# One pair of key tiles for both layers and two more SBUF pieces, with the order of all engines redone

## The chip, the cores and the metric

The kernel runs on one core of one Trainium2 chip. The time is the device time of one execution in microseconds. The core has a matmul engine (TensorE, PE in the profile), three engines for everything else (VectorE or DVE, ScalarE or ACT, GpSimd or POOL) and a queue, SyncE or SP, that issues all the DMAs here. The matmuls' sums lie in PSUM, eight banks of 128 x 512 floats; all other tiles lie in SBUF, 128 partitions wide.

## The reference

One inference step of two layers, for a prompt of 512 tokens and for 8 sequences of one new token each with 512 tokens in caches. 520 tokens go through each layer together. The reference, cut to its frame:

```python
for l in range(DEPTH):                       # 2 layers; prompt and samples alike
    h = rmsnorm(x, w_norm[l])
    a_val, a_gate, z_a, b_in, z_b, q, kv, gate, z_c = split(h @ w_in[l])
    q = rope(rmsnorm(q, g_q));  k = rope(rmsnorm(k, g_k))          # 8 query, 2 key heads, 3 branches
    y_a = conv_mixer(a_val * sigmoid(a_gate))                      # depthwise width 31, layer norm, 256 x 256
    y_b = pool_mixer(b_in)                                         # trailing means over 2, 4, 8, 16
    o_c = attention over blocks compressed by a small MLP (32 rows, stride 16)
    o_s = attention over the 8 best blocks of 64 rows
    o_w = attention over a window of 256 rows
    o = gate0 * o_c + gate1 * o_s + gate2 * o_w
    x = x + concat(y_a * silu(z_a), y_b * silu(z_b), o * silu(z_c)) @ w_out[l]
```

For the prompt there are at most 8 blocks of 64 rows, so the selection takes all of them. For the samples the window, the compressed rows and the selected rows come from caches: `cache_win_kv`, and `cache_cmp_kv` and `cache_slc_kv` through a page table (4 pages of 128 rows for each sequence).

## The kernel before, in words

All values are kept with channels on the partitions and the 520 tokens along the row. A float32 product is made exact enough with two rounded halves: `split` (L727) writes the value rounded to float32r, the high half, and the rest, the low half; `product` (L747) then makes three matmuls of 128 x 128 weights by 260 tokens for each of two halves of the tokens, so a group of six for each of 8 input chunks, and 48 for one product of 128 output channels. Each product fills two PSUM banks. 24 such products for each layer are the input projection (`proj`, from `w_in`) and 8 the output (`out`, L1375, from `w_out`). The projections are made on x without its norm; `evac` (L761) multiplies their sums with the norm of each token when it takes them out of PSUM. That norm comes from `norm` (L780) and `spread` (L698): sums of squares on PE, a reciprocal root in ten small DVE operations, a store of the 520 values to DRAM (a tile called `rs`), and a read back to all partitions.

The steps of a layer (L1412) are: the norm; keys and values of three branches (`key`, `value`); the compression of cached pages (`cmp_pages` loads 16 pages for each of two halves of the sequences, `compress` is matmuls of 160 or fewer columns); queries; attention for four blocks of 128 prompt queries (`attend`, L1180); convolution and its layer norm (`conv_norm`, L1073); pooling; the decode for two times four sequences (`decode`, L1270); and the output products.

In `decode` four window tiles' loads (`in_win`) feed the scores `s2`, and 16 page loads (`in_slc`) the scores `s1`. DVE and ACT make the softmax of both; PE transposes the result (seven transposes, in two sets), copies of these out of PSUM are the weights of 28 products, and one last transpose gives the four sequences' rows.

`attend` reads the keys of the selected and of the window branch as one row of 1088 columns: 512 keys of a branch and 32 compressed ones, two times. `key` and `cmp` write them, as a high and a low half. Before, each layer has two such tiles of its own (L589, L797).

**What sets the order.** The program is first recorded, step by step, as 3,330 numbered units (`Plan.add`), each one instruction or a burst of matmuls. The table `"order"` (L395) is a permutation of those numbers, and every engine and the SP queue get their instructions in that order (`emit`, L326); each engine runs its own list strictly in order. A second table, `"engines"` (L386), has a letter for each of 776 operations that more than one engine can do (copies out of PSUM, roundings, subtractions, scalings): v for DVE, s for ACT, g for POOL (`Choice.put`, L168). `place` (L286) walks through the order and gives each tile a piece of a region of SBUF, or a PSUM bank, that is free at that point, the one that has been free longest. So the order also decides which earlier tile an operation waits for. The regions stand at L383, as width in columns and number of pieces: region b, of 1040 columns, holds the attention rows of `attend` (`pr`), the cache loads of `decode` (`kvt`), a tile of compressed values (`vcd`) and the compression weights (`w1`).

Of the kernel before, what the change touches and what calls it, by code (L numbers as in the profile page):

```python
# [9 lines left out]
F32R = mybir.dt.float32r  # L10
# [179 lines left out]
class Plan:  # L190
# [135 lines left out]
    def emit(self, tc, ctx):  # L326
# [27 lines left out]
L = 2  # L354
# [32 lines left out]
        "vsssvvssgsssgssssvsgsgvvsgvgsvsssvgvvsgvvgggssvvvssvgvsvvvvvsvvvvvsvvvvvgvvsvvvvvssgggsvvvvgsggvsvssgvvsvsgsgssg"  # L387
        "vvsgggsvssvvvsggsvsvvgsvsvsvggsgssvggvvvggsssgsvvsvsvggvgggsvsvvvvgsvsvsgvgsvggsvvgggssssssvsvvggsggvsgggggvsgsg"
        "gvssvgvgvgsvsgvsvsvvssssssssgvgsvsvgvgvvvvvgvvvvgvssggggsgsvsgsvgvsssvssvsssssssssgsggvvvgvvvggvvvssvvsvvvgsssss"
        "vsvsvsvsgsgggsvgvgvvgvsgsvsvvvvvsgsvvgvvsvvgvvsvvvvvsssvvgvvsvgsvvsvsgvgsgvvsggvvgssvsvvvggsvvggsssvvvggggsgvvvv"  # L390
        "svvvsvsvvsvsgvvgvvgvvssvvvvssgvvvgvvsgvvvgvsggvsvsvvvvsggvsvssvvvsvvgvgggvsvsvsgsgggvsssvgsvssvvgvvvvvsssvvvgsgg"
        "gsvggggvgsggvvssgvvsgsvgsvvsvsssvsvggsvvgvsggvvgvgsggsvssgssgsggssssvvssssvssvvvgggsvgvggggvgsvvvsggvgggssssvgsv"
        "svggsvvvvsssvvsvssvvssvvvgvggvvgvggvggssvssvsgsvssvssvvsggvvgvvsvgvvvvvgsgsvsgsvsvsvgvsgggsvvgsggvgvsgsg"
    ),
    "order": (  # L395
# [147 lines left out]
def step_kernel(ctx: ExitStack, tc: tile.TileContext, i, o, tune=None):  # L543
# [176 lines left out]
    def layer(l):  # L720
# [63 lines left out]
        def rotate(src, dst):  # L784
# [7 lines left out]
            else:  # L792
                ch("vg").tensor_tensor(dst[0], t[:, :S], sh[:, :S], OP.add)
                ve.tensor_tensor(dst[1], t[:, S:T], sh[:, S:T], op=OP.add)

        z_.vs = {}
        kh, kl = keys[l]  # L797

        def kv_tiles():
            z_.knew, z_.vnew = new("knew", [128, 2, NB]), new("vnew", [NB, 2, 128])  # L800
# [756 lines left out]
```

## Time and profile before

| | before |
|---|---|
| median of 3 runs | 615.49 us (615.11 to 616.38) |
| the profiled execution | 617.24 us |
| its span in the trace | 615.5 us |
| PE busy | 601.9 us, 98% |
| DVE, ACT, POOL busy | 451.9, 259.6, 205.8 us |
| DMA | 90.99 MB, mean 148 GB/s |
| TensorE's granted clock | full in all of 40 slices |

The span goes from the first to the last instruction of the trace; the rest of the execution lies around it. PE's matmuls overlap each other, so its busy time is the time in which at least one is under way. Where a row ends in brackets, they hold the time the engine stood still before it, and what ended that.

### The profile page before, as it was taken

The page shows a single profiled execution, that of the slowest core. Times are in us where ns is not written, and L with a number is a line of the kernel's source. Part 1 is how long each engine was busy: PE and PEld are TensorE (multiplying, and loading weights), DVE is VectorE, ACT ScalarE, POOL GpSimd, SP SyncE. Part 2 cuts the span into 40 slices and gives each one's busy share as a digit, 9 for nine tenths or more (in the row PEclk, how much of TensorE's full clock was granted, in tenths as well). Part 3 has the DMA queues.
Part 4 walks back from the last instruction along what each step waited for, and adds up shares of the span by engine and source line. Part 5 has one row for each costly group of instructions (what it writes and reads, how often), then busy time and mean ns, then how long its engine had stood idle before and what let it go on. Part 6 is the DMA issues. An engine that isn't in the chain of part 4 may idle for free.

```text
span 615.5 us, 15050 instructions
## 1 busy us (share of the span) xinstructions
PE 601.9 (98%) x5542; PEld 538.0 (87%) x5542; DVE 451.9 (73%) x1264; ACT 259.6 (42%) x736; POOL 205.8 (33%) x224
## 2 busy tenths in 40 slices
PE   9989999999999999999999999999999999998997
PEld 8988999998788797679999999999986969677997
DVE  5465899988768887874573698898987598798411
ACT  5001135586664965520110220327846878424100
POOL 2211325633452354040502023443441444523330
PEclk9999999999999999999999999999999999999999
DMA  8574554214742456774854632532245315878951
GB/s 283 165 227 134 179 162 151 87 60 109 175 96 79 122 165 210 229 233 145 160 186 151 190 105 85 161 104 72 67 115 124 87 49 147 210 242 256 184 138 69
DMA packets 89131, 90.99 MB, mean 148 GB/s; under 512 B 25858, under 2 KB 59746, under 8 KB 88930
## 3 DMA queue, kind: packets, MB, share of 16 engines
q1 hardware_dynamic: 89058, 90.04, 50.8%
q8 instruction: 43, 0.70, 0.5%
q14 instruction: 30, 0.25, 0.1%
HBM read 75.32 MB, written 14.67 MB: 146 GB/s over the span
## 4 chain that ended last, share of the span: by engine, by line
PE 49%; DVE 2%; DMA 2%; SPq 1%; ACT 1%; issue 1%; POOL 0%; DVEq 0%; POOLq 0%
PE banks L352 49%; DVE t L352 1%; DMA t<-in_win 1%; SPq L352 1%; ACT t L352 1%; DMA t<-in_w_out 1%; DVE small L352 1%; POOL t L352 0%; ACT small L352 0%; DVEq L352 0%; POOLq L352 0%
## 5 line engine op out<-in xcount | busy, mean ns | idle before, releaser
L352 PE MATMUL banks<-t,t 128*128 128x260 f32 (+5 forms) x3976 | 483.5, 300 | 2.8 <-DVE t L352 1.8
L352 PEld LDWEIGHTS banks<-t,t 128*128 128x128 f32 (+3 forms) x3976 | 435.3, 177 | 35.1 <-issue 24.7
L352 POOL TENSOR_TENSOR t<-t,t 128x512 fp32r<-128x512 f32 (+4 forms) x78 | 102.2, 1315 | 161.1 <-PE banks L352 67.8
L352 ACT ACTIVATE t<-t 128x512 fp32r<-128x512 f32 (+4 forms) x125 | 75.2, 616 | 157.7 <-DVE t L352 68.6
L352 ACT ACTIVATE t<-t,small 128x384 f32<-128x384 f32 (+4 forms) x188 | 100.2, 549 | 12.5 <-DVE small L352 11.4
L352 DVE TENSOR_TENSOR t<-t,t 128x512 fp32r<-128x512 f32 (+4 forms) x108 | 75.3, 708 | 19.3 <-POOL t L352 8.7
L352 PE MATMUL banks<-keep,t 128*128 128x128 f32 (+8 forms) x698 | 86.6, 311 | 2.6 <-DVE t L352 2.3
L352 PEld LDWEIGHTS banks<-keep,t 64*128 64x128 f32 (+3 forms) x698 | 66.4, 161 | 18.3 <-issue 9.5
L352 DVE TENSOR_TENSOR t<-banks,t 128x520 f32<-128x520 f32 (+1 forms) x54 | 37.2, 694 | 50.2 <-PE banks L352 39.2
L352 DVE CUSTOM_DVE_ANT_0 t<-banks,keep,small 128x384 f32<-128x384 f32 (+3 forms) x128 | 64.0, 529 | 12.7 <-PE banks L352 12.1
L352 POOL TENSOR_SCALAR t<-t 128x512 fp32r<-128x512 f32 (+2 forms) x45 | 35.5, 790 | 95.3 <-DVE t L352 26.8
L352 ACT ACTIVATE t<-banks 128x512 f32<-128x512 f32 (+3 forms) x76 | 38.1, 516 | 41.2 <-PE banks L352 31.9
L352 PE MATMUL banks<-t,keep 128*32 128x130 f32 (+7 forms) x688 | 38.4, 299 | 2.3 <-DVE keep L352 0.8
L352 POOL TENSOR_SCALAR t<-t,small 128x384 f32<-128x384 f32 (+3 forms) x46 | 29.1, 645 | 25.5 <-DVE small L352 21.4
L352 PEld LDWEIGHTS banks<-t,keep 128*32 128x32 f32 (+3 forms) x688 | 22.5, 116 | 11.7 <-issue 3.4
L352 ACT ACTIVATE small<-small 128x32 f32<-128x32 f32 (+2 forms) x75 | 23.0, 309 | 18.3 <-DVE small L352 15.6
L352 DVE COPY t<-banks 128x512 f32<-128x512 f32 (+2 forms) x35 | 20.5, 592 | 13.3 <-PE banks L352 12.9
L352 DVE CAST t<-t 128x512 fp32r<-128x512 f32 (+2 forms) x48 | 20.7, 432 | 11.0 <-DMA t<-in_w_in 6.1
L352 DVE SCALAR_TENSOR_TENSOR small<-small 128x130 f32<-128x130 f32 (+3 forms) x80 | 27.7, 347 | 1.3
L352 DVE TENSOR_TENSOR small<-small 128x130 f32<-128x130 f32 (+6 forms) x66 | 26.9, 408 | 0.9
L352 POOL TENSOR_TENSOR t<-t,keep 128x520 f32<-128x520 f32 (+1 forms) x9 | 12.9, 1439 | 37.5 <-DVE t L352 36.8
L352 ACT ACTIVATE t<-t,keep 128x520 fp32r<-128x520 f32 (+2 forms) x17 | 14.3, 842 | 25.7 <-DVE t L352 11.0
(81 smaller groups left out, 370.2 us busy)
## 6 DMA issues: line engine op xcount, KB each, us to landing
t<-in_w_in SPq DMA_DIRECT2D x96, 256.0 KB, 2.9
t<-in_cmp SPq DMA_DIRECT2D x64, 128.0 KB, 2.6
t<-in_slc SPq DMA_DIRECT2D x64, 128.0 KB, 2.3
t<-in_w_out SPq DMA_DIRECT2D x32, 256.0 KB, 3.7
t<-in_x SPq DMA_DIRECT2D x16, 260.0 KB, 4.6
t<-in_win SPq DMA_DIRECT2D x16, 256.0 KB, 3.6
out_win<-t SPq DMA_DIRECT2D x16, 256.0 KB, 5.5
t<-glu SPq DMA_DIRECT2D x12, 264.0 KB, 5.6
```

The lines of the kernel that those rows point to most:

```text
L352: fn(*[real(v) for v in o.a], **{k: real(v) for k, v in o.k.items()})
```

## The change

It keeps one pair of key tiles (high and low half, 1088 columns each) that both layers write and read, instead of a pair for each layer. That frees 2 x 1088 columns of each partition, and region b gets two more pieces of 1040. The tables of the engines and of the order are new: 399 of the 776 letters differ, with 282 operations on DVE, 273 on ACT and 221 on POOL where there were 315, 256 and 205, and the order is another permutation of the same units.

```diff
-    "regions": {"s": (32, 111), "u": (552, 38), "b": (1040, 10), "d": (2560, 5)},
+    "regions": {"s": (32, 111), "u": (552, 38), "b": (1040, 12), "d": (2560, 5)},
...
     "engines": (
-        "vsssvvssgsssgssssvsgsgvvsgvgsvsssvgvvsgvvgggssvvvssvgvsvvvvvsvvvvvsvvvvvgvvsvvvvvssgggsvvvvgsggvsvssgvvsvsgsgssg"
...
+        "vsvssssgvgssssssvvgvgggvvvggsgvsssgssgvvsssgssvsvgggsvsvsvvvsgsvggssvvvgggvgvsggvssvvggvsgvgsggvsvssgvvsvvvsvssv"
...
-    keys = [[new("kk", [128, 1088], F32R, fixed=True) for k in range(2)] for l in range(L)]
+    keys = [new("kk", [128, 1088], F32R, fixed=True) for k in range(2)]
...
-        kh, kl = keys[l]
+        kh, kl = keys
```

What the new order makes of two places:

PE at the start of layer 0, where the first compression matmuls begin. A row `128x260 x2` is one third of a group of six projection matmuls (t_186 and t_330 are the two halves of a chunk of x, t_452 and t_514 the halves of weights), a row `128x2x80` is a compression matmul. Before:

```order
L352 MATMUL banks<-t_186,t_476 128x260 x2
L352 MATMUL banks<-t_330,t_476 128x260 x2
L352 MATMUL banks<-t_186,t_484 128x260 x2
L352 MATMUL banks<-t_196,t_452 128x260 x2
L352 MATMUL banks<-t_332,t_452 128x260 x2
L352 MATMUL banks<-t_196,t_514 128x260 x2
L352 MATMUL banks<-t_231,t_229 128x2x80
L352 MATMUL banks<-t_231,t_528 128x2x80
```

After the change (t_551 and t_586 are the weights of a fifth product):

```order
L352 MATMUL banks<-t_377,t_465 128x260 x2
L352 MATMUL banks<-t_559,t_465 128x260 x2
L352 MATMUL banks<-t_377,t_467 128x260 x2
L352 MATMUL banks<-t_104,t_551 128x260 x2
L352 MATMUL banks<-t_134,t_551 128x260 x2
L352 MATMUL banks<-t_104,t_586 128x260 x2
L352 MATMUL banks<-t_220,t_327 128x2x80 x4
L352 MATMUL banks<-t_220,t_604 128x2x80
```

Before, 29 groups of six stand ahead of the first compression matmul, the fourth of the four products that are open then not yet whole. Now all four are whole, 32 groups, and the first group of a fifth product comes next, then the compression.

SP in layer 1, where the loads for the decode begin: `in_win` are the windows of two sequences to a tile, `in_slc` cached pages, `in_w_pw` the pointwise weights, `rs` the read of the layer norm's rows. Before:

```order
L352 DMA t949_7123<-rs5879_76 128x520
L352 DMA t951_7142<-in_w_pw 128x512
L352 DMA t955_7157<-in_win 128x512
L352 DMA out_pool_s<-small_84 1024x1x15
L352 DMA t955_7157<-in_win 128x512
L352 ISA
L352 DMA t959_7200<-in_slc 128x256
L352 ISA
L352 DMA t959_7200<-in_slc 128x256
L352 DMA t966_7234<-in_win 128x512 x2
```

After the change:

```order
L352 DMA t914_6878<-in_win 128x512 x2
L352 DMA t916_6912<-in_w_in 128x512
L352 DMA t924_6943<-in_win 128x512
L352 DMA t928_6962<-in_w_in 128x512
L352 DMA out_kv<-small_84 128x8
L352 DMA out_conv_p<-small_84 128x30
L352 DMA t939_7010<-in_w_in 128x512
L352 DMA t940_7012<-in_w_pw 128x512
```

The four window loads of the first half of the decode stood behind the pointwise weights, the last two behind pages too. Three of them stand ahead of those weights now, and the fourth, which is not shown, three rows behind the read of `rs`.

## Rows read from the trace of the kernel before

**Rows 1.** The page's first part: busy us, share of the span, instructions.

```profile
PE 601.9 (98%) x5542; PEld 538.0 (87%) x5542; DVE 451.9 (73%) x1264; ACT 259.6 (42%) x736; POOL 205.8 (33%) x224
```

**Rows 2.** Busy time by stage: stretch, length, busy us of each engine, clock, DMA.

```profile
70.00:220.00 150.00, 150.00 (x1421) 130.63 (x1421) 126.32 (x409) 92.38 (x288) 60.73 (x66) 1.00 0.41 115
280.00:520.00 240.00, 239.87 (x2205) 218.96 (x2204) 179.28 (x522) 102.14 (x304) 78.11 (x86) 1.00 0.43 120
```

**Rows 3.** PE's timeline, 0 to 70 us: start, us, instruction, [idle before <-releaser].

```profile
34.37 1.35 PE L352 MATMUL banks<-t,t 128*128 128x160 f32 x8 [1.77 <-DVE t L352]
...
60.45 9.77 PE L352 MATMUL banks<-t,t 128*128 128x160 f32 x76 [1.08 <-DMA t<-in_cmp]
```

**Rows 4.** DVE's timeline, 22 to 36.5 us.

```profile
33.62 1.31 DVE L352 TENSOR_TENSOR t<-banks,t 128x520 f32<-128x520 f32 x2 [1.49 <-DMA t<-rs]
```

**Rows 5.** SP's timeline, 16 to 60 us: start, us of issuing, DMA.

```profile
25.18 0.66 SPq L352 DMA_DIRECT2D rs<-small  x1
25.89 0.38 SPq L352 DMA_DIRECT2D t<-in_w_in  x1
...
28.67 0.37 SPq L352 DMA_DIRECT2D t<-rs  x1
...
55.32 2.56 SPq L352 DMA_DIRECT2D t<-in_cmp  x3
```

**Rows 6.** PE's timeline at the end of layer 0, 226 to 276 us.

```profile
229.85 2.81 PE L352 MATMUL banks<-keep,t 128*128 128x128 f32 x24 [0.68 <-DVE t L352]
244.73 1.36 PE L352 MATMUL banks<-t,keep 128*32 128x512 f32 x6 [0.47 <-DVE small L352]
...
264.14 2.45 PE L352 MATMUL banks<-t,t 128*128 128x260 f32 x18
...
266.45 2.40 PE L352 MATMUL banks<-t,t 128*128 128x260 f32 x18
270.28 0.63 PE L352 MATMUL banks<-keep,t 128*128 128x128 f32 x4 [1.43 <-DVE t L352]
```

**Rows 7.** DVE and POOL in the same place, 262 to 271 us.

```profile
264.61 2.67 POOL L352 TENSOR_TENSOR t<-t,t 128x520 fp32r<-128x520 f32 x2 [1.02 <-ACT t L352]
265.89 0.16 DVE L352 TENSOR_TENSOR t<-banks,small 128x2 f32<-128x2 f32 x1
266.09 1.22 DVE L352 TENSOR_SCALAR small<-small 128x2 f32<-128x2 f32 x1
269.44 0.69 DVE L352 TENSOR_SCALAR t<-t,small 128x512 f32<-128x512 f32 x1
```

**Rows 8.** PE's timeline at the end of layer 1, 518 to 616 us.

```profile
532.01 0.64 PE L352 MATMUL banks<-t,keep 128*32 128x256 f32 x8 [0.61 <-DMA t<-in_win]
549.28 0.66 PE L352 MATMUL banks<-keep,t 128*128 128x128 f32 x4 [0.20 <-POOL t L352]
553.62 1.14 PE L352 MATMUL banks<-t,small 128*128 128x260 f32 x4 [0.34 <-DVE t L352]
556.56 0.65 PE L352 MATMUL banks<-t,keep 128*32 128x128 f32 x16 [0.75 <-DVE keep L352]
557.44 0.42 PE L352 MATMUL banks<-t,keep 33*32 33x128 f32 x8 [0.23 <-ACT keep L352]
565.91 1.14 PE L352 MATMUL banks<-t,small 128*128 128x260 f32 x4 [0.57 <-ACT t L352]
```

**Rows 9.** SP's timeline from 500 us, and the landing in the chain that ended last.

```profile
514.82 0.33 SPq L352 DMA_DIRECT2D t<-rs  x1
525.21 0.82 SPq L352 DMA_DIRECT2D t<-in_win  x2
525.60 6.37 DMA t<-in_win
```

**Rows 10.** Groups of instructions by shape: count, busy us, mean ns of one, idle before.

```profile
L352 PE MATMUL banks<-t,t 128*128 128x260 f32 x3120 | 406.1, 287 | 0.0
L352 DVE TENSOR_TENSOR t<-t,t 128x512 fp32r<-128x512 f32 x80 | 57.1, 722 | 16.8 <-POOL t L352 8.7 <-issue 3.7 <-ACT t L352 2.0
L352 POOL TENSOR_TENSOR t<-t,t 128x512 fp32r<-128x512 f32 x66 | 86.8, 1321 | 142.5 <-PE banks L352 64.2 <-DVE t L352 31.1 <-issue 22.0
```

More of the change, by code (lines that the diff above doesn't have):

```diff
@@ L386 @@
     "engines": (
-        "vsssvvssgsssgssssvsgsgvvsgvgsvsssvgvvsgvvgggssvvvssvgvsvvvvvsvvvvvsvvvvvgvvsvvvvvssgggsvvvvgsggvsvssgvvsvsgsgssg"
[L388 to L393, printed above, removed]
+        "vsvssssgvgssssssvvgvgggvvvggsgvsssgssgvvsssgssvsvgggsvsvsvvvsgsvggssvvvgggvgvsggvssvvggvsgvgsggvsvssgvvsvvvsvssv"
+        "vvsgsvgvssvvvsvggvgvggsgsvsgsvsgggsssvvgsgvvgvsvsvssssvsvsgsgvvsvvvggvvgggssgssvvsgggsssssssssvvgsvgvsggsvsvsgvg"
+        "vsvgvsvvgsgsvsssssvsssssssssgvvgggvsvgvggvsvgsvgsvssvsgsvsgggsssgvsssvvsssvsssvssvvggvgvvsvvvvvgvvsvsvsvvgsvvsss"
+        "vgvsgvgsggvvvsgvggsvsgsgsvvgggsvgvsvsgggggvgsvsgvvggssvvgvsgsvsgsgsgsggvvgvggvsvsssvsvsvsggvvsvgvsvsvsgvvvgvsvvv"
+        "svsvggsvvvgvvvvvvvvggsvvvgsssgvgsvsvggssvvvsggvsvvvvvgvgsvggsvvggsvggvgvvvvvsgsvsgvggssvvsggvggvsvgvssssssgsvsgs"
+        "ggvgvgggvgggvsvsvvssvsggvsssvssssvvggvgvgsggvggvsvgsgsssgvggvssssssvssssvsvssvvsggggvsvsvvggggsvvsggvvvgvgssgggs"
+        "sgvvgvssvsssvssssssvvgvsgvggvsvvvvgvvsvsvsvssvgsvvssssvggsgsvsggvvgvvgsvsvsgsgvgsvgvgvvgsvsvvggvsvsgggvg"
     ),
     "order": (
[141 rows of a table removed]
[141 rows of a table added]
     ),
```

282 rows, old and new, of the table TUNE are left out of this document.

## The prediction

> **What bounds the kernel now.** The page's first part comes first: TensorE (PE) is busy for 601.9 of a span of 615.5 us, VectorE (DVE) for 451.9, and the other two compute engines for less than half [rows 1]. So any order of the same work can win back at most the 13.6 us in which PE stands still, and part of that is the start before the first matmul and the tail after the last. The table by stage tells where the stops are: from 70 to 220 us PE is busy for 150.00 of 150.00 us and from 280 to 520 us for 239.87 of 240.00 [rows 2]. What is left to win lies in three places, and PE's timeline gives it stop by stop, in brackets behind the row:
>
> - The start of layer 0: 1.77 us before the first compression matmul and 1.08 us before the second half of the compression [rows 3].
> - The end of layer 0, with the decode: 0.68, 0.47 and 1.43 us [rows 6].
> - The end of layer 1, with the decode: 0.61, 0.20, 0.34, 0.75, 0.23 and 0.57 us [rows 8].
>
> These eleven stops are 8.13 us. Everything else in the change can only make new stops, or change how fast PE runs through its own list.
>
> **The change part by part.**
>
> *One key pair.* It removes no instruction. It adds a wait: layer 1 may write its keys only after layer 0 has read its last ones. The keys of layer 1 come out of projections that need all eight output products of layer 0, and those need its whole attention, so the reads are over before the first write can be asked for. Cost nothing; the cover is the dependency itself, and no order can take it away.
>
> *PE's own list.* The change adds and removes no matmul. The listing of PE's order has 2,325 groups of like rows before and 2,336 after, so there are some more places at which one kind follows another. The trace has no row for such a place alone. A 260-column matmul takes 406.1/3120 = 0.130 us in the mean, its places of change included [rows 10], and not even a whole one is likely to be lost per added place, so 11 places cost at most 11 x 0.13 = 1.4 us. The same listing could as well have cheaper neighbours, so I keep -1.4 as the other end. I take nothing.
>
> *Start of layer 0.* At 32.60 us PE is ready for the first compression matmul, and it starts at 34.37 [rows 3]. The row names DVE: all eight PSUM banks hold sums of projections, and the first is freed when DVE multiplies it with the norm, which waits for the rows read back from DRAM ("rs") and starts at 33.62 [rows 4]. That round trip hangs in SP's queue, which issues in order: the store goes out at 25.18 and the read at 28.67, with four other issues between [rows 5]. In the new order 32 groups of six projection matmuls stand ahead of the first that needs a freed bank, against 29 before: 18 x 0.13 = 2.3 us more cover. Against that, one more cache page and one more weight load are issued ahead of the store, three issues instead of four stand between store and read, and DVE has two more subtractions in its chain: I put the read's landing some 1 us later. What is left of 1.77 is 1.77 - 2.3 + 1 = about 0.4 us. For the second stop, PE gets 48 projection matmuls more (312 against 264) and two half-size compression matmuls fewer ahead of it, some 48 x 0.13 = 6.2 us, less half a microsecond. The last page that it needs is issued five SP issues later, and an issue there takes 0.4 to 0.9 us (three took 2.56) [rows 5], so 2 to 4.5 us. PE itself comes 1.4 us earlier from the first stop. 5.7 - 1.4 = 4.3 us later at PE against 2 to 4.5 us at the page: the 1.08 goes away. Gain 1.4 + 1.1 = 2.5 us. The bounds are 2.85 us, if both vanish, and a loss of 1.5 us, if the page is late by the whole 4.5 and the read by 2.
>
> *End of layer 0.* The stop of 1.43 us is the softmax of the second four sequences. Its last scores end before 264.14, PE fills the wait with 36 output-product matmuls (18 and 18) [rows 6], and DVE delivers the scaled row at 269.44 + 0.69 [rows 7]. The new order puts 42 there: 6 x 0.13 = 0.8 us less stop. The 0.47 and the 0.68 have the same neighbours as before and stay. Gain 0.8; bounds 1.4 and 0, as nothing is taken out of that chain.
>
> *End of layer 1.* The 0.61 us is a load that comes late: the window keys of two sequences are issued at 525.21, because the piece of SBUF that they go to held attention rows until then, and land 6.37 us later [rows 9]. With 12 pieces of 1040 columns instead of 10, three of the four window loads stand ahead of the pointwise weights, and the fourth three issues behind the LayerNorm rows, whose read goes out at 514.82 before [rows 9]: 10 us earlier than the late one. Gain 0.6. The 0.20 us has 48 projection matmuls and four small ones ahead of it instead of 42: 0.8 us more cover, gone. The 0.75 and 0.23 us stand between the last transposes and their products; four small matmuls, six projection matmuls and the pooling product now stand there instead of six projection matmuls, so they go too. The 0.57 us is a bank that waits for ScalarE's exponential; the new order gives the pooling product a bank that is freed by an earlier read, so it goes. The 0.34 us stays. One stop is new: the last seven transposes and the 28 products behind them had six matmuls between them and now have none, so the products wait for a copy out of PSUM, some 0.5 us (as the 0.23 and 0.75 us stops behind such copies [rows 8]). Gain 0.6 + 0.2 + 1.0 + 0.6 - 0.5 = 1.9 us; bounds 2.7 and 0.
>
> *The choice of engines.* 399 of 776 choices differ; DVE gets 33 operations fewer, ScalarE 17 and GpSimd (POOL) 16 more. A subtraction takes 0.72 us on DVE and 1.32 on POOL [rows 10]. POOL is idle for two thirds of the span and PE's stops name it once, so I cost the move at nothing; its cover is PE's projection work, and if that is gone each moved subtraction on PE's path costs 0.6 us. POOL can also hold DVE up: a DVE operation on 2 columns that otherwise takes 0.16 us took 1.22, up to the end of a POOL subtraction that had begun before it, in the very chain that ends in the 1.43 us stop [rows 7].
> The Trainium skill, page "SBUF — State Buffer", section "Who interferes with whom", says more: DVE and GpSimd share one pair of ports as an exclusive lock, and whoever comes second is blocked for the other's whole instruction. The trace agrees in the 1.22 us row. By that rule 16 more POOL operations could hold DVE for 16 x 1.32 = 21 us, as an estimate, about what 33 fewer operations free on it; the time by it would lie between my forecast and the first rival's.
>
> *New stops.* Nearly every row of every engine has moved, so stretches that had no stop can get one. The trace of before cannot show them. I allow two of the mean size, 8.13/11 = 0.74, together 1.5 us; the bounds are none, and eight of them, 6 us.
>
> Sum: 2.5 + 0.8 + 1.9 - 1.5 = 3.7 us less. The profiled execution took 617.24 us with a span of 615.5; the median of the runs shown is 615.49. The difference is taken off the median: 615.49 - 3.7 = **611.8 us**.
>
> **The rivals.**
>
> *POOL holds the chains (slower).* The place: the softmax chains of the decode and the weight splits where DVE is busy, each ending in something PE waits for. The price: 1.0 us for each small DVE operation caught behind a POOL subtraction [rows 7]. For it: it happened in the longest stop of layer 0's end, and there are 16 more POOL operations. Against it: POOL's time is idle for the most part [rows 1], and of the decode chains two get more PE cover, while only the last gets less (24 projection matmuls and some small ones instead of 36). Four such catches use up the forecast gain; eight make 611.8 + 8 = 619.8 us.
>
> *The cover moves, the time doesn't (no change).* In the late stretches PE waits for DVE, SP and DMA at once; if the store of the norm's rows and the last page slip as much as PE's arrival does, the 2.5 us are not won, and the 1.9 us shrink to the window load's 0.6. Then 615.49 - 0.6 - 0.8 + 1.5 = 615.6 us. Here belongs that the two pieces are not used by the late loads at all; the listing speaks against it.
>
> *All cover holds (much faster).* No new stops and nine of the eleven gone, all but 0.68 and 0.34: 615.49 - 7.1 = 608.4 us. For it: DVE loses 33 operations. Against it: the bounds above would have to be met all together.
>
> **How the numbers follow.** Forecast, 609.5 to 614.2: 0.50. Much faster, under 609.5: 0.14. No change: 0.13. Slower: 0.23. A measurement of this kernel can tell about 0.2%, 1.2 us, from no change. So faster is 0.64, the same 0.13, slower 0.23. The range goes from 607.5 to 618.5, which leaves out about 0.05 below and 0.1 above; the forecast's own range is 609.5 to 614.2.
>
> **What would show it.** PE busy stays within 1.4 us of 601.9. PE's timeline: the stop before the first compression matmul is under 1 us and the next one gone; the stop before the layer 0 transposes is about 0.6 us; no stop for in_win; a stop of some 0.5 us before the last 28 decode products. DVE's busy time falls by 10 to 20 us. I am wrong if PE's idle time is 13 us or more, above all if stops appear between 70 and 220 or 280 and 520 us, or if many small DVE operations take over 1 us.

## The result, and the profile after

| | before | changed |
|---|---|---|
| median of 12 runs | 615.91 us (614.73 to 619.74) | 619.20 us (616.63 to 624.16) |
| ratio to before, 95% interval | | 1.0064 (1.0039 to 1.0089) |
| profiled execution, its span | 617.24, 615.5 us | 618.12, 616.0 us |
| mean granted clock, by execution | 1.000 (profiled) | 0.988 to 0.997, median 0.994 |

The change is slower by 0.64%; 611.8 us with a range up to 618.5 was predicted. The page's first part for the changed kernel:

```profile
PE 599.8 (97%) x5542; PEld 537.9 (87%) x5542; DVE 440.3 (71%) x1231; ACT 266.8 (43%) x753; POOL 218.9 (36%) x240
```

Against [rows 1], PE is busy 2.1 us less and DVE 11.6 us less, but PE stands still for 616.0 - 599.8 = 16.2 us instead of 13.6. The stops come from PE's timelines of the changed kernel (start, us, instruction, idle before it and what ended it):

```profile
35.09 3.58 PE L352 MATMUL banks<-t,t 128*128 128x260 f32 x26 [0.77 <-DVE t L352]
...
246.86 0.96 PE L352 MATMUL banks<-keep,t 128*128 128x128 f32 x7 [1.84 <-DVE t L352]
...
385.04 0.99 PE L352 MATMUL banks<-t,t 128*128 128x260 f32 x6 [1.67 <-DVE t L352]
...
489.91 0.44 PE L352 MATMUL banks<-t,keep 128*64 128x128 f32 x4 [1.86 <-ACT t L352]
...
523.85 0.66 PE L352 MATMUL banks<-keep,t 128*128 128x128 f32 x4 [1.49 <-ACT t L352]
...
525.36 1.09 PE L352 MATMUL banks<-t,keep 128*64 128x128 f32 x16 [0.86 <-ACT t L352]
...
550.25 1.02 PE L352 MATMUL banks<-keep,t 128*128 128x128 f32 x4 [2.07 <-ACT t L352]
...
559.70 1.14 PE L352 MATMUL banks<-t,small 128*128 128x260 f32 x4 [0.48 <-DVE t L352]
```

The stops that the prediction counted are nearly all gone: of the 1.77 us of [rows 3] 0.77 are left, a stop like the 0.34 of [rows 8] is 0.48, and the 1.08, 0.68, 0.47, 1.43, 0.61, 0.75, 0.23 and 0.57 don't exist any more. But six stops of 0.86 to 2.07 us are new or grown, 9.8 us together. Two of them stand where there was one of about 0.2 us: the 0.20 of [rows 8], and in layer 0 this one, which the prediction did not count:

```profile
252.00 0.96 PE L352 MATMUL banks<-keep,t 128*128 128x128 f32 x7 [0.19 <-DVE t L352]
```

The others stand where [rows 2] had shown PE busy with hardly a break, or in the last attention block. The table by stage of the changed kernel shows two of them (stretch, length, busy us of PE, its weight loads, DVE, ACT and POOL, granted clock, DMA), and one thing more:

```profile
70.00:220.00 150.00, 149.90 (x1417) 132.67 (x1416) 124.84 (x404) 98.75 (x303) 56.60 (x67) 1.00 0.45 123
280.00:520.00 240.00, 236.22 (x2174) 214.84 (x2173) 174.77 (x509) 101.83 (x305) 85.05 (x93) 1.00 0.47 124
550.00:554.00 4.00, 3.75 (x19) 3.75 (x20) 2.12 (x7) 1.78 (x5) 0.00 (x0) 0.57 0.34 116
```

Between 280 and 520 us PE now stands still for 3.78 us instead of 0.13. And behind the longest stop, at 550 us, TensorE's granted clock falls to its lower level, 1.2 instead of 2.4 GHz; over the 4 us of this row the mean is 0.57. In the profile of the kernel before it is full in all 40 slices, and in the 65 executions of that kernel beside the experiments its mean was 0.999 or more in 61 and 0.997 in four.

Why the new stops are so long shows on the engine that PE waits for. DVE at 384 us, then ACT and POOL at 489 and 523 us:

```profile
381.68 0.76 DVE L352 SCALAR_TENSOR_TENSOR t<-t,keep,t 128x520 f32<-128x520 f32 x1 [3.06 <-DMA t<-rs]
...
384.30 0.69 DVE L352 TENSOR_TENSOR t<-banks,t 128x520 f32<-128x520 f32 x1
...
486.06 1.21 ACT L352 ACTIVATE t<-t,keep 128x512 f32<-128x512 f32 x1 [1.84 <-DMA t<-cv]
...
521.17 1.29 POOL L352 TENSOR_TENSOR t<-t,t 128x520 f32<-128x520 f32 x1 [5.36 <-DMA t<-rs]
...
522.49 0.82 ACT L352 ACTIVATE t<-t,small 128x520 f32<-128x520 f32 x1 [3.99 <-POOL t L352]
...
523.22 0.58 ACT L352 ACTIVATE t<-banks 128x512 f32<-128x512 f32 x1
```

Three times an engine stands at the head of its queue waiting for a row that is read back from DRAM, directly or through POOL, and behind that operation, in order, stands the copy out of PSUM that PE needs. At 384 us the sums had been complete for some 3 us when DVE took them out: in PE's list their last group of six is the seventh of the ten that run from 375.92 to 383.38 us, so they ended near 381 us, as an estimate.

The other two, at 247 and 550 us, are the softmax chains of the first four sequences of each layer:

```profile
245.16 2.07 DVE L352 TENSOR_SCALAR t<-t,small 128x512 f32<-128x512 f32 x2
245.17 1.26 POOL L352 TENSOR_TENSOR t<-t,t 128x512 fp32r<-128x512 f32 x1 [0.79 <-PE banks L352]
...
542.22 1.39 POOL L352 TENSOR_TENSOR t<-t 64x524 f32<-64x524 f32 x1
542.62 1.03 DVE L352 TENSOR_SCALAR small<-keep,small 128x8 f32<-128x8 f32 x1
...
547.90 1.26 POOL L352 TENSOR_TENSOR t<-t,t 128x512 fp32r<-128x512 f32 x1
548.25 0.94 DVE L352 TENSOR_TENSOR t<-t,keep 64x16 f32<-64x16 f32 x1
```

The operations on 8 and on 16 columns end when POOL's ends beside them (543.65 and 543.61, 549.19 and 549.16 us). The first of them takes 1.03 us, where its like took 0.22 in the kernel before. That is the pattern of [rows 7].

So the theory after the result: the new tables leave PE in five places with less work than the wait is long; its stops there are copies queued behind waits, and chains held by POOL; and the stops also bring TensorE's clock down, in some executions more often than in the profiled one. The rivals: the memory part costs something, the choice of engines does it all, or the clock falls for another reason than the stops.

### The profile page after: what moved, and what is told of

It is laid out like the page before. It is cut to its first block, busy times and chain, and to the rows that moved or that the text cites. A ratio compares the mean times of both kernels' runs of the same rounds, so it can differ in the third digit from the quotient of the medians.

```text
span 616.0 us, 15075 instructions
## 1 busy us (share of the span) xinstructions
PE 599.8 (97%) x5542; PEld 537.9 (87%) x5542; DVE 440.3 (71%) x1231; ACT 266.8 (43%) x753; POOL 218.9 (36%) x240
## 5 line engine op out<-in xcount | busy, mean ns | idle before, releaser
L352 PE MATMUL banks<-t,t 128*128 128x260 f32 (+6 forms) x3976 | 483.2, 300 | 2.6 <-DVE t L352 2.4
L352 POOL TENSOR_TENSOR t<-t,t 128x512 fp32r<-128x512 f32 (+4 forms) x80 | 105.4, 1323 | 155.7 <-PE banks L352 56.5
L352 ACT ACTIVATE t<-t 128x512 fp32r<-128x512 f32 (+5 forms) x131 | 78.3, 610 | 140.3 <-DVE t L352 44.8
L352 DVE TENSOR_TENSOR t<-t,t 128x512 fp32r<-128x512 f32 (+3 forms) x106 | 78.6, 748 | 18.3 <-ACT t L352 7.4
L352 PEld LDWEIGHTS banks<-keep,t 128*128 128x128 f32 (+3 forms) x698 | 66.3, 162 | 23.6 <-ACT t L352 7.9
L352 ACT ACTIVATE t<-banks 128x512 f32<-128x512 f32 (+3 forms) x89 | 44.1, 512 | 44.4 <-PE banks L352 29.4
L352 POOL TENSOR_TENSOR t<-t 128x520 f32<-128x520 f32 (+2 forms) x13 | 15.8, 1217 | 36.9 <-DVE t L352 22.3
L352 DVE SCALAR_TENSOR_TENSOR t<-t,t 128x520 f32<-128x520 f32 (+2 forms) x32 | 23.9, 758 | 5.4 <-ACT t L352 5.2
L352 ACT ACTIVATE small<-small 128x32 f32<-128x32 f32 (+3 forms) x78 | 23.9, 309 | 7.0 <-DVE small L352 7.0
L352 DVE SCALAR_TENSOR_TENSOR t<-t,keep,t 128x520 fp32r<-128x520 f32 (+1 forms) x22 | 19.4, 894 | 10.2 <-DMA t<-rs 9.1
```

Source lines behind the costliest of these rows:

```text
L352: fn(*[real(v) for v in o.a], **{k: real(v) for k, v in o.k.items()})
```

## The experiments

**The memory part alone.** The change without its two tables.

```diff
-    "regions": {"s": (32, 111), "u": (552, 38), "b": (1040, 10), "d": (2560, 5)},
+    "regions": {"s": (32, 111), "u": (552, 38), "b": (1040, 12), "d": (2560, 5)},
...
-    keys = [[new("kk", [128, 1088], F32R, fixed=True) for k in range(2)] for l in range(L)]
+    keys = [new("kk", [128, 1088], F32R, fixed=True) for k in range(2)]
```

> The memory of the change alone: one key pair and 12 pieces, with the order and the letters of before. My account (the change is slower because its new order stops PE for 1.5 to 2.1 us at a time, and TensorE's granted clock then falls): same as before, 615.9 us within 1, granted clock as high as before's. Rival (the shared key pair or the moved pieces cost something themselves): 617 us or more.

Measured: 613.66 us, ratio 0.9953 (0.9932 to 0.9974), clock 0.999 to 1.000 in eight executions. It is faster, which neither account had said. PE's list is the same unit by unit, so its timeline shows where:

```profile
32.76 1.52 PE L352 MATMUL banks<-t,t 128*128 128x160 f32 x8 [0.45 <-DVE t L352]
...
59.67 10.64 PE L352 MATMUL banks<-t,t 128*128 128x160 f32 x83 [1.06 <-DMA t<-in_cmp]
...
267.90 0.63 PE L352 MATMUL banks<-keep,t 128*128 128x128 f32 x4 [0.37 <-DVE t L352]
```

The 1.77 and 1.43 us of [rows 3, 6] are 0.45 and 0.37, and the stop for the window load and the 0.57 us of [rows 8] are gone. The 1.08 stays as 1.06, and stops of 0.41 and 0.80 us are new, at 56 and 417 us.

**One key pair, still 10 pieces.**

```diff
-    "regions": {"s": (32, 111), "u": (552, 38), "b": (1040, 12), "d": (2560, 5)},
+    "regions": {"s": (32, 111), "u": (552, 38), "b": (1040, 10), "d": (2560, 5)},
```

> The kernel before with one key pair and still 10 pieces, its own order and letters: the sharing alone. My account (sharing costs and brings nothing, the two more pieces bring the gain of the memory part): the same as before, ratio 0.998 to 1.002, the window load's stop of 0.6 us in layer 1 still there. Rival (the gain comes from where the tiles lie, or from the shared pair): ratio near 0.995 as with 12 pieces.

Measured: 617.24 us beside 616.71 before, ratio 0.9996 (0.9980 to 1.0012). The window load's stop is there, and so are 1.74 and 1.33 us at the other two places:

```profile
533.36 0.64 PE L352 MATMUL banks<-t,keep 128*32 128x256 f32 x8 [0.44 <-DMA t<-in_win]
```

Sharing the pair costs and brings nothing that this ratio shows; the two pieces bring the gain.

**The new order with the old letters, and the old order with the new letters**, both with the memory of the change. In each, one table is put back:

```diff
-        "vsvssssgvgssssssvvgvgggvvvggsgvsss...
+        "vsssvvssgsssgssssvsgsgvvsgvgsvsssv...
```

```diff
-        "17 16 2 116 36 28 18 40 34 79 4 5...
+        "2 4 5 17 6 7 16 79 36 8 81 9...
```

> The change with the letters of before: memory and new order, old choice of engines. My account: the order alone makes the long stops, so the clock falls here too (mean 0.998 or less) and the time is 617 to 622 us. Rival (16 more POOL operations hold DVE and make the stops): with the old letters the stops go, the clock stays at 1.00 and the time is under 615 us.

> The change with the order of before: memory and new letters, old order. My account: few long stops, as the order is what places PE's cover; 615 to 618 us with the clock at 0.998 or more. Rival (the letters are what hurts, through POOL): 618 us or more with stops behind DVE operations that POOL holds up.

Measured: 650.93 us, ratio 1.0558 (1.0529 to 1.0588), and 648.03 us, ratio 1.0505 (1.0474 to 1.0537). My account missed both, by some 30 us; the rival's "618 us or more" for the letters holds by its number, and PE's longest stop there, 4.89 us at 65 us, is one that POOL ends. PE stands still for 35 us (652.8 - 617.6) and 37 us (649.1 - 611.7), in some 40 stops, and the mean clock is 0.984 to 0.996. These two runs can't tell which table does the harm: each, with the other's old partner, is far worse than the two together.

**Idle matmuls in three of the stops.** A constant matrix is multiplied with itself, into the bank that the waiting instruction is about to overwrite.

```diff
+    def fill(unit, n):
+        u = plan.units[unit]
+        bank = [b for b in u.ops[0].bufs if b.kind == "psum"][0]
+        dst = View(bank, _BACK[:, :512], (), F32)[:, :128]
...
+            o.eng, o.fn, o.a, o.k = "tensor", "matmul", (dst, mean_w, mean_w), {"start": True, "stop": True}
...
+    fill(1437, 5)
+    fill(2718, 5)
+    fill(3085, 6)
     plan.place([int(v) for v in tune["order"].split()])
```

> The changed kernel with idle matmuls (5, 5 and 6 pairs of 128 columns, 0.28 us a pair, whose result is overwritten) put on PE inside three of its long stops, before the transposes at 246.9 us, before the product at 489.9 and before the transposes at 550.3. They fit in the wait, so no stop gets longer or shorter for the work behind it. My account (the clock falls because PE stands still): granted clock 0.997 or more in nearly every run instead of 0.994, no fall behind the stop at 550, and 616.0 to 617.5 us instead of 619.2. Rival (the clock falls for another reason, or its falls cost nothing): 619 us as the changed kernel, the clock at 0.994.

Measured: 617.73 us, a little over the range that I had given, ratio 1.0014 (0.9997 to 1.0032), just clear of the changed kernel's 1.0064 (1.0039 to 1.0089). The median clock is 0.997, in two executions 1.000. Its four executions at 0.999 or more took 616.4 to 617.9 us, beside a median of 617.0 for the kernel before next to it, so at a full clock the changed kernel with these fillings is about as fast as the kernel before. In the wait at 550 us PE stands still for 0.55 us instead of 2.07, and the clock does not fall behind it:

```profile
550.00:554.00 4.00, 3.45 (x30) 3.26 (x29) 3.54 (x10) 2.31 (x5) 0.62 (x1) 1.00 0.55 186
```

What a fall costs can be read from the rows of the same 18 matmuls behind that stop, first of the changed kernel, then of this one, there with the four transposes ahead of them:

```profile
550.92 3.69 PE L352 MATMUL banks<-t,t 128*128 128x260 f32 x18
```

```profile
551.72 0.66 PE L352 MATMUL banks<-keep,t 128*128 128x128 f32 x4 [0.55 <-ACT t L352]
552.13 2.40 PE L352 MATMUL banks<-t,t 128*128 128x260 f32 x18
```

They differ by 1.29 us, and the four transposes take 1.02 against 0.66: 1.65 us for one fall. In the profiled execution one is left, behind a stop without a filling:

```profile
524.38 0.92 PE L352 MATMUL banks<-keep,t 128*128 128x128 f32 x4 [1.92 <-ACT t L352]
```

**A longer stop in a kernel without falls.** The other direction, on the memory part alone.

```diff
+    def again(unit, n):
+        u = plan.units[unit]
+        first, ops = u.ops[0], []
...
+            o.eng, o.fn, o.a, o.k = first.eng, first.fn, first.a, first.k
...
+    again(3088, 6)
     plan.place([int(v) for v in tune["order"].split()])
```

> The memory part alone (613.7 us, clock 0.999 to 1.000, no stop over 1.1 us), with one copy that PE waits for in layer 1's decode made seven times by DVE instead of once, to the same place with the same values: its stop of 0.75 us grows to some 2.5 us, nothing else is changed. Account with the clock (a stop of this length makes the granted clock fall behind it): a fall to 0.50 behind the stop in most executions, mean clock 0.997, and 616.5 to 617.5 us, 1.75 for the stop and 1.7 for the fall. Rival (the falls of the changed kernel come from something else than its stops): clock 0.999 or more and 615 to 615.6 us.

Measured: 616.45 us, ratio 0.9981 (0.9962 to 1.0001). The stop in the memory part alone, and then DVE's and PE's timelines of this kernel's profiled execution:

```profile
555.12 0.64 PE L352 MATMUL banks<-t,keep 128*32 128x128 f32 x16 [0.75 <-DVE keep L352]
```

```profile
552.35 1.77 DVE L352 COPY keep<-banks 128x64 f32<-128x64 f32 x7
```

```profile
554.17 1.00 PE L352 MATMUL banks<-t,keep 128*32 128x128 f32 x24 [2.30 <-DVE keep L352]
```

This execution is one of four with the clock at 0.999 or more; in eight of twelve it is 0.997 or 0.994. The memory part alone was at 0.999 or more in all of its eight executions, and the kernel before, next to this one, in 16 of 17. So a stop of this length brings the clock down in most executions, not in all. What the stop costs by itself is less clear: it is 1.55 us longer, and at a full clock the median is 614.38 us, only 0.7 above the 613.66 that the memory part alone took on another chip. By the clock of the execution, the medians of four kernels are (the last two are the next two experiments):

| mean granted clock | changed | longer stop | copies ahead of waits | POOL's four moved |
|---|---|---|---|---|
| 0.999 to 1.000 | none | 614.38 (4) | 614.72 (4) | 614.20 (5) |
| 0.996 to 0.997 | 618.12 (3) | 616.64 (6) | 616.20 (8) | 615.35 (4) |
| 0.993 to 0.994 | 619.09 (5) | 618.56 (2) | none | 616.92 (3) |
| 0.988 to 0.992 | 622.34 (4) | none | none | none |

From one row to the next, where 0.003 of the clock is 0.003 x 616 = 1.8 us, the time rises by 1 to 3 us in each column. By the numbers of executions, in brackets, the changed kernel is the only one of the four that never ran with a full clock.

**Copies ahead of waits** in the changed kernel, at 384, 489 and 523 us. A line is a unit's place in the order.

```diff
-2049 DVE, on the rows read back
-2050 DVE, on 2049
...
 2073 DVE, takes the query sums out of PSUM
+2049
+2050
...
 2716 PE, transposes
+2717 ACT, copies them out
+2713 ACT, scaling of a row
+2712 ACT, the same
+2704 ACT, the same
...
+2917 ACT, copy out of PSUM
+2922 ACT, copy out of PSUM
 2823 ACT, on the layer norm's rows
```

> The changed kernel with eight units moved: a copy out of PSUM that PE waits for goes ahead of an operation of the same engine that waits for a DMA, in three places (DVE at 384 us, ScalarE at 489 and at 523 us). My account (each of these stops is a copy queued behind an engine's wait for a read-back): the stops of 1.67, 1.86, 1.49 and 0.86 us shrink to under 0.6 in all, the clock stays at 0.997 or more, and the time is 614 to 616.5 us, ratio 0.997 to 1.001. Rival (PE waits there for something else as well, so the stops only move): 618 us or more, clock 0.994.

Measured: 616.16 us, ratio 0.9981 (0.9967 to 0.9995), clock 0.996 to 1.000. The stop at 384 us is gone, but of the others more is left than the 0.6 us that I had said:

```profile
485.39 2.40 PE L352 MATMUL banks<-keep,t 128*128 128x128 f32 x18 [1.38 <-ACT t L352]
...
524.19 3.94 PE L352 MATMUL banks<-t,t 128*64 128x512 f32 x14 [1.64 <-DVE t L352]
```

5.88 us became 3.02: PE met the next copy in the same queue, at 485 us still behind the wait for the convolution's read-back, at 524 behind another DVE product. A stop of 0.96 us, at 539 us, is new in this profile. Against the changed kernel the ratio falls from 1.0064 to 0.9981, and the intervals don't touch.

**POOL's operations beside the chains** given to others, one of them moved behind the chain.

```diff
-    letter 365: g    (subtraction at 245 us)
+    letter 365: v
-    letter 345: g    (scaling behind it)
+    letter 345: s
-    letter 696: g    (subtraction at 540.7 us; its unit 2957 moved behind 3080)
+    letter 696: v
-    letter 738: g    (subtraction at 547.9 us)
+    letter 738: v
```

> The changed kernel with four POOL operations that run beside the two first softmax chains of the decode given to DVE or ScalarE, one of them moved behind the chain. My account (POOL's operations hold up small DVE operations of the chains, 1.0 us at 245 us and about 1.7 us at 542 to 549 us): the stops of 1.84 and 2.07 us fall to under 1.0 and 0.6 us, and the time by 1.5 to 3 us, to 616.5 to 618 us, ratio 1.001 to 1.004. Rival (the chains are long by themselves): stops as in the changed kernel, 619 us.

Measured: 615.03 us, ratio 0.9972 (0.9952 to 0.9993), more than expected. DVE's two scalings of 2.07 us are one row of 0.63, the operation on 8 columns takes 0.22 us instead of 1.03, and the two stops are 0.76 and 0.48:

```profile
245.54 0.63 DVE L352 TENSOR_SCALAR t<-t,small 128x512 f32<-128x512 f32 x2
...
544.27 0.22 DVE L352 TENSOR_SCALAR small<-keep,small 128x8 f32<-128x8 f32 x1
```

```profile
246.17 0.95 PE L352 MATMUL banks<-keep,t 128*128 128x128 f32 x7 [0.76 <-DVE t L352]
...
550.43 0.66 PE L352 MATMUL banks<-keep,t 128*128 128x128 f32 x4 [0.48 <-ACT t L352]
```

The profiled execution has two falls of the clock, at stops that this edit did not touch: behind the one at 385 us, 1.88 us here, and behind two short ones, 1.24 us at 524 us and this one, after which the 16 matmuls take 1.75 us that took 1.09 in the changed kernel:

```profile
525.74 1.75 PE L352 MATMUL banks<-t,keep 128*64 128x128 f32 x16 [0.86 <-ACT t L352]
```

**Both together**, the two edits above in one kernel.

> The moves of the one and the letters of the other together. My account (six long stops make the whole loss, by themselves and through the clock): no stop over 1.2 us behind the start, the clock at 0.998 or more, 611 to 614 us, ratio 0.992 to 0.997, which is at or under the memory part alone. Rival (the new tables lose in many small places): 615 us or more with a clock that is full.

Measured: 611.93 us, ratio 0.9923 (0.9906 to 0.9940). It beats both kernels of the case. Against what I had said, two stops over 1.2 us were left: one of 1.36 us at 525 us, and a longer one, behind which the clock fell in the profiled execution: the same 18 matmuls take 3.45 us here that took 2.40 above.

```profile
484.67 3.45 PE L352 MATMUL banks<-keep,t 128*128 128x128 f32 x18 [2.05 <-ACT t L352]
```

**Two more copies ahead of waits** on top of that.

```diff
-2604 ACT, on the convolution's read-back
...
 2717 ACT, copies transposes out
+2604
...
+2919 DVE, copies transposes out
 2786 DVE, on ACT's gate
```

> The last version with two more moves: ScalarE's copy that frees PE's transposes at 484 us goes ahead of the operation that waits for the convolution's read-back, and DVE's copy at 524 us ahead of a product that waits for ScalarE. My account (what is left of the loss is copies behind waits): the stops of 2.05 and 1.36 us fall to under 0.5 us each, the clock stays full, and the time falls by 1.5 to 3 us to 609 to 610.5 us, ratio 0.987 to 0.990. Rival (PE is short of work there, the stop moves on): 611 to 612 us as before the moves.

Measured: 611.41 us, ratio 0.9897 (0.9872 to 0.9923), clock 0.999 or more in all six executions. The stop of 2.05 us is 0.56 and 0.46 now, but the one of 1.36 is 0.77 and 0.97, and the time is the rival's, not mine: PE's waiting there mostly moved on.

```profile
484.51 2.40 PE L352 MATMUL banks<-keep,t 128*128 128x128 f32 x18 [0.56 <-ACT t L352]
488.33 2.88 PE L352 MATMUL banks<-keep,t 64*128 64x512 f32 x20 [0.46 <-ACT t L352]
...
523.76 1.94 PE L352 MATMUL banks<-t,t 128*64 128x512 f32 x8 [0.77 <-ACT t L352]
526.67 1.07 PE L352 MATMUL banks<-t,t 128*64 128x512 f32 x2 [0.97 <-ACT t L352]
```

The two ratios' intervals overlap, so it is not shown that this step brings anything over the one before. By the ratios the two are 1.4 and 1.7% under the changed kernel, with nine and eleven of 3,330 units moved and four letters changed.

## Why the prediction was wrong

- **The terms that were read from rows held by their size, and in part by luck.** Start of layer 0, end of layer 0 and end of layer 1: of the eleven stops, 8.13 us, 0.77 and 0.48 remain, and the one of 0.20 us has become 2.07. I had taken 5.2 us of gain; it was 8.13 - 0.77 - 0.48 = 6.9 us, with the 2.07 us in place of the old 0.20 counted under the new stops. The window load's stop went, and the memory part alone shows that the two pieces do it: with 10 of them it comes back. But the two pieces also take 1.77 to 0.45 and 1.43 to 0.37 us with the old order, so the reason that I gave for these two, more matmuls ahead of the wait, is not shown. The 0.68 and 0.47, which I had left standing, went as well, and the stop of some 0.5 us that I expected in front of the last 28 products didn't come.
- **The 0.20 us** was said to go because more matmuls would stand ahead of it. They do, 48 instead of 42, and it grew all the same: from the start of those matmuls to the transposes behind the softmax it took 550.25 - 541.81 = 8.4 us, and 549.28 - 543.77 = 5.5 before. With POOL's four operations moved it is 550.43 - 543.57 = 6.9. I had counted PE's cover and taken the chain's length as given. The matmuls before, and in the changed kernel:

```profile
543.77 5.31 PE L352 MATMUL banks<-t,t 128*128 128x260 f32 x42
```

```profile
541.81 6.01 PE L352 MATMUL banks<-t,t 128*128 128x260 f32 x48
```

- **The step that failed is "New stops".** I allowed two of the mean size, 1.5 us, with 6 us as the bound. They are 9.8 us. Of the signs that I had named for being wrong, two came in full: PE stands still for 16.2 us, over the 13, and there are stops between 280 and 520 us. An allowance by the mean size of the old stops was the error: the old stops were those that a fitted order had left, and with a new order and new letters a stop has the size of whatever wait lies at the head of a queue. The same view that gave the terms could have bounded it: a read-back takes 4.9 us from issue to landing (33.6 against 28.67 [rows 4, 5]), and whatever stands behind its reader can wait as long.
- **The step that was missing is the clock.** [Rows 2] show it at 1.00, and I took that as given. The median clock of the changed kernel is 0.994, so 0.006 x 618 = 3.7 us of clock, and the medians differ by 619.20 - 615.91 = 3.3 us. In the profiled execution, with one fall of 1.65 us, the difference is only 618.12 - 617.24 = 0.9 us: 9.8 us of new stops and the fall, less 6.9 us of old stops and 3.7 us of PE's own list, which is the next point. The fillings and the longer stop show that stops bring the falls, in most executions and not in all.
The Trainium skill, page "TensorE: Matmul & The Clock Gate", Part 1, says that a monitor sets the clock by how busy PE has been recently, and that the window in which it looks is free-running and doesn't start with the kernel. The executions agree with both: with the same longer stop the mean clock is 0.997 or less in eight of twelve and full in four.
- **PE's own list**, taken as 0 with bounds of 1.4 us: the changed kernel's PE is busy for 599.8 us with 1.65 us of a fall in it, 598.2 without, 3.7 us less than before. The kernel with copies ahead of waits has 599.4 us at a full clock, the one with two more of them 600.1; with the old tables the one with 10 pieces has 602.6 and the memory part alone 601.5. So the new list is shorter by 1 to 4 us in these single profiles, in most pairs more than my bound; why, no run tells.
- **The choice of engines**, costed at nothing: wrong in the two chains. The slower rival had this mechanism, but it looked to the last chain of the decode; the stops are in the first chain of each layer, and at the second of layer 0, where PE's cover grew as I had said, the 1.43 us are gone. Giving four operations away brings 0.9% by the ratios. The rule of the Trainium skill, page "SBUF — State Buffer", section "Who interferes with whom", that of DVE and GpSimd, where both need the ports that they share, the second is blocked for the other's whole instruction, is what the rows show at 542 and 548 us, where the held operation ends with POOL's. But the rival's 1 us for a catch left out the clock that a lengthened stop can cost on top.
- **The key pair** at no cost: right, ratio 0.9996 (0.9980 to 1.0012).
- **DVE's busy time** fell by 11.6 us, as said (10 to 20), and it did not help: what PE waits for is not DVE's sum of work but its order.

## What to carry to other kernels

Where PE is the bound and its clock is full, a stop costs up to its length and sometimes a fall on top (here 1.65 us); look at the mean clock of all executions, not only of the profiled one. When a change moves the order, ask of each wait not only what covers it but whether the chain behind it gets longer. When an order is redone, walk the queue of each engine that frees PE's banks and ask what stands ahead of each copy: an operation that waits for a read-back, or for another engine that does, should stand behind it. Tables that were fitted together are judged together, and a part of a change that is free by itself, here two more pieces of SBUF, is worth measuring alone before anything is fitted to it.

## What the runs showed of the hardware that was not expected

- A stop of 2.30 us brought the granted clock down in most executions of one program and not in the rest. The length of the stop alone does not decide: in the profiles the clock fell behind stops of 1.88, 1.92, 2.05 and 2.07 us and behind a pair of 1.24 and 0.86, and not behind that of 2.30, nor behind those of 1.84 and 1.86.
- Tenths of a microsecond can decide whether POOL or DVE goes first. In the kernel before, a DVE operation on 2 columns took 1.22 us behind a POOL subtraction [rows 7]; with the two more pieces and the same order it began 0.18 us earlier relative to POOL, took 0.17 us, and POOL's two subtractions took 2.95 instead of 2.67:

```profile
264.76 0.17 DVE L352 TENSOR_SCALAR small<-small 128x2 f32<-128x2 f32 x1
```

```profile
263.46 2.95 POOL L352 TENSOR_TENSOR t<-t,t 128x520 fp32r<-128x520 f32 x2 [1.03 <-ACT t L352]
```

- The first read-back of the norm's rows landed 4.9 and 4.8 us after its issue in the two kernels with 10 pieces and 3.7 us in the two with 12 and the old order, at the same place in the same queue. That is what shortened the first stop from 1.77 to 0.45 us; why it lands earlier stays open, and no run was made for it.
